# A hybrid decoder layer in fp32: the sum of two weight tiles of w_out, w_up and w_down formed in SBUF instead of DRAM

## The chip, the cores and the metric

The kernel runs on one core of a Trainium2 chip. The metric is the device time in microseconds (us) of one execution. Before the change the median of three runs is 1453.36 us (1452.56 to 1453.89).

## What is computed

One decoder layer (Hymba style) on 256 tokens with a model width of 2048, everything in float32:

```
u   = rmsnorm(h, norm_mix_pre)
P   = u @ w_in                       # 2048 x 12320: z | x,B,C | dt | q | k | v
y   = concat(SSD(z, xBC, dt), attention(q, k, v))       # 256 x 4096
h   = h + rmsnorm(y @ w_out, norm_mix_post)             # w_out 4096 x 2048
hdn = relu(rmsnorm(h, norm_mlp_pre) @ w_up) ** 2        # w_up 2048 x 8192
h   = h + rmsnorm(hdn @ w_down, norm_mlp_post)          # w_down 8192 x 2048
```

The SSD part is a chunked state space scan with a short causal convolution, the attention a mixture of three dilations. The four large products with w_in, w_out, w_up and w_down make up most of the work; all their weights are read from DRAM once.

## The kernel before, in words

**Products in two parts.** TensorE multiplies in a reduced fp32 format (F32R). To keep float32 accuracy each operand is split into a rounded part hi and a remainder lo, and three products stand for one: hi·hi, lo·hi and hi·lo. For the weights the split is made on the way: a *raw* tile of 2 x 128 rows by 512 columns (512 KB) is loaded by SP, ScalarE writes hi (L147), VectorE writes lo (L148), and TensorE uses both. There are five buffers each of hi and lo (BUFS).

**Plain steps and sevens.** The kernel works on two blocks of 512 columns at a time (a *unit*), over steps k of 256 rows. A plain step (row_tiles, row_tile, L331 to L333) loads one raw tile for each column block and makes 12 products of 128 x 128 x 512 from each: 24 for the two. A *seven* (seven(), L386 to L420) does the same step by a scheme of Strassen and Winograd with seven block products instead of eight: 21 products. It needs sums of blocks of weights. With raw_a the tile of the first column block and raw_b that of the second (each of rows [:, 0] and [:, 1]), raw_b's first half must hold the sum of its two row blocks, and VectorE then forms

```
e[:, 1] = raw_a[:, 0] + raw_b[:, 0]
e[:, 0] = e[:, 1] - raw_b[:, 1]
t4      = e[:, 1] + raw_a[:, 1]
```

through add_in_line, whose instructions are recorded at L252. The first of them is called e1 in what follows. The helpers split_in_line and add_in_line chain the instructions: on VectorE and ScalarE each stands behind the one before it, in the order e1, e[:, 0], split of raw_a, t4, split of e, split of raw_b, split of t4.

**Where the sum of raw_b's rows comes from.** plan() (L265) writes the order of the steps of each unit, and enters every seven in the list pairs. next_pair() (L270) takes the next entry and has GpSimd (POOL) make the sum in DRAM: a copy of the first 128 x 512 block to one of five places in DRAM (L279), then a transfer of the second block that adds onto it (L280, accum_op). Each of these is 256 KB, and POOL waits for the first to land before it issues the second. This runs four pairs ahead (PAIRS_AHEAD). fetch() (L152) then loads the finished sum into raw_b's first half (L156) and the second row block, unchanged, into its second half (L157); any other raw tile is one transfer (L161). There are 87 sevens: 21 in the products with w_in (z, q and k, v), 12 in w_out, 28 in w_up and 26 in w_down.

**The ring of raw tiles.** fetch_next() (L212) gives out the raw tiles in turn: the four of the pool wp (RAWS) and those that a stage adds in room["raw"], which are tiles that are free there: two more in w_out (part of uc), four more in the first half of w_up (the mw tiles, from the ninth raw tile on, since the turn starts at -2 * RAWS), one more in the first half of w_down (mw2), three more in the second half of w_up (ha), five more in the second half of w_down (uc and ha). A raw tile is loaded again when its last reader (hi, lo or one of the sums) has ended; SP issues the loads in order and waits at each for its slot.

**The orders.** In w_up each unit has sevens at k = 1, 3, 4 and 6. In the first half of w_down the two units are (4, 6, 9, 10, 11 and 13 are sevens in the first, 4, 6, 9, 11, 13, 10 and 8 in the second):

```
plan(("down", 0), w_down, 0, (0,1,2,4,3,6,5,9,7,10,8,11,12,13), (4,6,9,10,11,13))
plan(("down", 0), w_down, 2, (0, 4, 1, 6, 2, 9, 11, 3, 13, 5, 10, 7, 8), (4, 6, 9, 11, 13, 10, 8))
```

so that most sevens have one plain step between them. The remaining steps of a unit (14 and 15, for instance) follow as plain steps. At the end of w_out and the start of w_up an order written out by hand (mix_to_up, L1115) holds all engines; there POOL makes four small powers (L1084).

Of the kernel before, what the change touches and what calls it, by code (L numbers as in the profile page):

```python
# [14 lines left out]
ALU = mybir.AluOpType  # L15

P = 128
# [21 lines left out]
NB = 512  # L39
KB = 2  # L40
# [37 lines left out]
def hymba_layer(ctx: ExitStack, tc: tile.TileContext, x, norm_mix_pre, w_in, conv_w, conv_b, dt_bias, a_log,  # L78
                d_skip, ssm_norm_w, w_out, norm_mix_post, norm_mlp_pre, w_up, w_down, norm_mlp_post,
                consts, out):  # L80
    nc = tc.nc
    w_in, w_out, w_up, w_down = w_in[0], w_out[0], w_up[0], w_down[0]
# [69 lines left out]
    def fetch(src, k0, c0, step=KB, into=None, pair=None):  # L152

        raw = wp.tile([P, KB, NB], F32, name="raw", bufs=RAWS) if into is None else into
        if pair is not None:
            nc.sync.dma_start(raw[:, 0], pair)  # L156
            loaded[:] = [nc.sync.dma_start(raw[:, 1], src[(k0 + 1) * P:(k0 + 2) * P, c0:c0 + NB])]  # L157
            return raw
        for j in range(0, KB, step):
            rs = slice((k0 + j) * P, (k0 + j + step) * P)  # L160
            loaded[:] = [nc.sync.dma_start(raw[:, j:j + step], src[rs, c0:c0 + NB].rearrange("(k p) n -> p k n", p=P))]  # L161
        return raw

    loaded = []
# [47 lines left out]
    def fetch_next(src, k0, c0, pair=None):  # L212

        turn = room["turn"]
        room["turn"] += 1
        n = turn % (RAWS + len(room["raw"])) - RAWS
        into = None if turn < 0 or n < 0 else room["raw"][n]
        with ExitStack() as order:
            for last in loaded if room.get("chain") else ():
                order.enter_context(tc.issue_after(last.ins))  # L220
            return fetch(src, k0, c0, into=into, pair=pair)
# [32 lines left out]
    pairs = []  # L254

    w_z, w_v, w_ups, w_downs = w_in[:, COL_Z:], w_in[:, COL_V:], [w_up[:, hf * 4096:] for hf in range(2)], [w_down, w_down[4096:]]
    orders = {}

    def order_of(ks, by_seven):
        return [(k, k in by_seven) for k in ks]  # L260

    def blocks_of(n):
        return n if isinstance(n, tuple) else (n * NB, (n + 1) * NB)

    def plan(name, src, n, order, by_seven):  # L265

        orders[name, n] = order_of(order, by_seven)
        pairs.extend((src, blocks_of(n), k) for k in order if k in by_seven)

    def next_pair():  # L270

        if not pairs:
            return
        src, (ca, c), k = pairs.pop(0)
        cb = slice(c, c + NB)
        d = places[len(paired) % len(places)]
        if len(paired) < len(places):
            nc.gpsimd.dma_start(d[:, 0:1], room["pairs"])
        nc.gpsimd.dma_start(d, src[k * KB * P:(k * KB + 1) * P, cb])  # L279
        nc.gpsimd.dma_start(d, src[(k * KB + 1) * P:(k * KB + 2) * P, cb], accum_op=ALU.add)  # L280
        paired.append((src, ca, k, d))
# [3 lines left out]

    def pair_of(src, ca, k):

        next_pair()
        s_, c_, k_, d = paired[turn_of["pair"]]
        assert (s_ is src) and (c_, k_) == (ca, k), (c_, k_, ca, k)  # L290
        turn_of["pair"] += 1
        return d
# [3 lines left out]
    def weights(src, k0, c0, fetch=fetch):  # L296

        with tc.high_priority(offset=AHEAD):
            raw = fetch(src, k0, c0)
            hi, lo = parts()  # L300
            if fetch is fetch_next:
                split_in_line(hi, lo, raw)
                return hi, lo
            line.clear()
            with ExitStack() as order:
                while behind:
                    order.enter_context(tc.issue_after(behind.pop().ins))
                split(hi, lo, raw)
        return hi, lo
# [76 lines left out]
    def seven(src, ca, cb, k, acc, more, first, last):  # L386
# [4 lines left out]
        with tc.high_priority(offset=AHEAD):  # L391
            raw_a = fetch_next(src, k * KB, ca)
            raw_b = fetch_next(src, k * KB, cb, pair_of(src, ca, k))
            e, t4 = sum_tile(), tmp()
            add_in_line(e[:, 1], raw_a[:, 0], raw_b[:, 0])
            add_in_line(e[:, 0], e[:, 1], raw_b[:, 1], ALU.subtract)
            hl_a = parts()
            split_in_line(*hl_a, raw_a)
            add_in_line(t4, e[:, 1], raw_a[:, 1])
            hl_e = parts()  # L400
            split_in_line(*hl_e, e)
            hl_b = parts()
            split_in_line(*hl_b, raw_b)
            hl_t = parts()
            split_in_line(*(v[:, 0] for v in hl_t), t4)
# [16 lines left out]
    def combine_new(dst, more):  # L422

        with tc.high_priority(offset=AHEAD):
# [6 lines left out]
            nc.vector.tensor_tensor(b[1], more[3], b[0], op=ALU.add)  # L431

    plan("z", w_z, 0, (0, 2, 4, 6, 1, 3, 5), (1, 3))
    plan("z", w_z, 2, (0, 2, 1, 4, 3, 6, 5), (1, 3, 5))
    qk_blocks = [(COL_Q + hb * NB, COL_K + hb * NB) for hb in range(3)]
    plan("qk", w_in, qk_blocks[1], (0, 2, 1, 4, 3, 5, 6), QK_SEVENS)
    plan("v", w_v, 0, range(7), V_SEVENS)
    plan("qk", w_in, qk_blocks[2], (0, 2, 1, 3, 4, 5, 6), QK_SEVENS)
# [513 lines left out]
    def keys_too(hb, pumps=(1,)):  # L952
        return queries(COL_Q + hb * NB, rbq, pumps), queries(COL_K + hb * NB, rbc, pumps)
# [76 lines left out]
    qk = [keys_too(0, (2, 1))]  # L1030
# [526 lines left out]
```

## Time and profile before

| | before |
|---|---|
| median of 3 runs | 1453.36 us |
| the profiled execution: span | 1451.4 us |
| TensorE (PE) busy | 1442.4 us, 99% |
| VectorE (DVE) busy | 1300.4 us, 90% |
| ScalarE (ACT) busy | 947.1 us, 65% |
| GpSimd (POOL) busy | 162.3 us, 11% |
| SP's transfers (q1) | 272.37 MB, 58.1% of 16 transfer engines' span |
| POOL's transfers (q0) | 45.63 MB, 15.7% |
| granted TensorE clock, mean | 0.999 |

The profile is of one execution, whose span of 1451.4 us is 2.0 us below the median of the runs. The stages overlap at their borders; by the issues of SP's transfers they run roughly so: w_in to 566 us, w_out from 568 to 745, the first half of w_up from 746, the first half of w_down from 918, the second half of w_up up to 1254, and the second half of w_down to 1422, with the output after it.

In the views, a line names the engine and the source line, then what it writes <- what it reads. Rows of a timeline begin with the start and the duration in us; "SPq" is SP's queue issuing a transfer, so its duration is that of the issue and not of the transfer. The time "to landing" is counted from the issue to the semaphore that tells of the data's arrival. Lists of waits give the total, the number and the longest. A wait in brackets at the end of a row is idle time of that engine just before it and what ended it.

### The profile page before, as it was taken

What the parts mean: (1) busy time and instruction counts of PE and PEld (TensorE: products, weight loads), DVE (VectorE), ACT (ScalarE), POOL (GpSimd) and SP (SyncE); (2) the same over time, 40 slices, a digit from 0 to 9 for tenths busy, and PEclk for the clock granted to TensorE, in tenths of its full rate; (3) what the DMA queues carried; (4) which work ended last, traced back from release to release, by engine and by line L of the source; (5) the groups of instructions that cost most, each with busy time, mean ns of one, the idle gap of its engine ahead of it and who ended that gap; (6) DMA issues with size and microseconds to landing.
All of it is one profiled execution on the core that took longest, in us unless ns stands there. A gap on an engine that the chain in (4) does not pass through costs nothing.

```text
span 1451.4 us, 20394 instructions
## 1 busy us (share of the span) xinstructions
PE 1442.4 (99%) x7042; PEld 1214.7 (84%) x7042; DVE 1300.4 (90%) x1881; ACT 947.1 (65%) x1351; POOL 162.3 (11%) x244
## 2 busy tenths in 40 slices
PE   9999999999999999999999999999999999999998
PEld 8888888888888888888888888888888888888886
DVE  7788888988999788689988999999889999999998
ACT  7577669665666666556657677656465776766664
POOL 0201110131111000010100011010111110101000
PEclk9999999999999999999999999999999999999999
DMA  8977656756898658588976798688888888788854
GB/s 267 272 219 222 189 175 187 239 170 195 231 253 248 196 127 244 173 270 257 280 225 217 210 311 240 203 221 251 249 255 279 255 245 247 210 293 265 248 179 160
DMA packets 172359, 332.97 MB, mean 229 GB/s; under 512 B 16048, under 2 KB 18976, under 8 KB 172256
## 3 DMA queue, kind: packets, MB, share of 16 engines
q1 hardware_dynamic: 144736, 272.37, 58.1%
q0 software_dynamic: 19648, 45.63, 15.7%
q10 hardware_dynamic: 7872, 13.68, 2.8%
q8 instruction: 55, 0.90, 0.3%
q14 instruction: 48, 0.39, 0.1%
HBM read 327.39 MB, written 49.84 MB: 260 GB/s over the span
## 4 chain that ended last, share of the span: by engine, by line
PE 76%; ACT 1%; DVE 1%; DMA 0%; issue 0%; ACTq 0%
PE acc L331 10%; PE acc L333 10%; PE acc L332 10%; PE acc L418 7%; PE acc L419 7%; PE acc L420 7%; PE acc L485 4%; PE ps L331 3%; PE ps L332 3%; PE ps L333 3%; PE ps L418 2%; PE ps L419 2%; PE ps L420 2%; PE acc L488 2%; PE acc L1463 1%; PE ps L938 0%
## 5 line engine op out<-in xcount | busy, mean ns | idle before, releaser
L148 DVE TENSOR_TENSOR lo<-raw,hi 128x1024 fp32r<-128x1024 f32 (+1 forms) x387 | 470.1, 1220 | 79.1 <-ACT hi L147 76.3
L147 ACT ACTIVATE hi<-raw 128x1024 fp32r<-128x1024 f32 (+1 forms) x387 | 404.2, 1050 | 204.2 <-PE acc L333 71.4
L485 PE MATMUL acc<-ua,hi 128*128 128x512 f32 x520 | 141.2, 401 | 0.1
L147 ACT ACTIVATE hi<-e 128x1024 fp32r<-128x1024 f32 x66 | 70.2, 1063 | 68.5 <-DVE e L252 62.7
L485 PEld LDWEIGHTS acc<-ua,hi 128*128 128x128 f32 x520 | 91.3, 189 | 14.2 <-ACT hi L147 0.2
L331 PE MATMUL acc<-hi,ua 128*128 128x512 f32 x228 | 90.6, 397 | 0.0
L332 PE MATMUL acc<-lo,ua 128*128 128x512 f32 x228 | 89.3, 392 | 0.0
L333 PE MATMUL acc<-hi,ua 128*128 128x512 f32 x228 | 89.2, 391 | 0.0
L331 PE MATMUL acc<-hi,sh 128*128 128x512 f32 x220 | 86.9, 395 | 0.0
L333 PE MATMUL acc<-hi,sl 128*128 128x512 f32 x220 | 85.8, 390 | 0.0
L332 PE MATMUL acc<-lo,sh 128*128 128x512 f32 x220 | 85.7, 390 | 0.0
L488 PEld LDWEIGHTS acc<-ua,lo 128*128 128x128 f32 x520 | 76.5, 190 | 8.9
L148 DVE TENSOR_TENSOR lo<-e,hi 128x1024 fp32r<-128x1024 f32 x66 | 80.5, 1220 | 0.0
L488 PE MATMUL acc<-ua,lo 128*128 128x256 f32 x520 | 78.8, 282 | 0.0
L419 PE MATMUL acc<-lo,ah 128*128 128x512 f32 x180 | 70.1, 390 | 0.0
L420 PE MATMUL acc<-hi,al 128*128 128x512 f32 x180 | 70.1, 390 | 0.0
L418 PE MATMUL acc<-hi,ah 128*128 128x512 f32 x180 | 70.1, 390 | 0.0
L485 PE MATMUL acc<-uc,hi 128*128 128x512 f32 x208 | 61.4, 405 | 0.0
L148 DVE TENSOR_TENSOR lo<-ha,hi 128x1024 fp32r<-128x1024 f32 x43 | 52.5, 1221 | 6.0 <-ACT hi L147 5.8
L147 ACT ACTIVATE hi<-ha 128x1024 fp32r<-128x1024 f32 x43 | 45.2, 1057 | 19.4 <-PE acc L333 12.4
L147 ACT ACTIVATE hi<-r 128x512 fp32r<-128x512 f32 x66 | 41.5, 629 | 20.8 <-PE acc L333 8.8
L418 PE MATMUL acc<-hi,ua 128*128 128x512 f32 x137 | 53.7, 392 | 0.0
(572 smaller groups left out, 3722.3 us busy)
## 6 DMA issues: line engine op xcount, KB each, us to landing
raw<-in_w_in_dram SPq DMA_DIRECT2D x154, 512.0 KB, 4.5
raw<-in_w_down_dram SPq DMA_DIRECT2D x69, 512.0 KB, 5.7
raw<-in_w_up_dram SPq DMA_DIRECT2D x65, 512.0 KB, 4.8
raw<-in_w_out_dram SPq DMA_DIRECT2D x38, 512.0 KB, 5.1
raw<-pair SPq DMA_DIRECT2D x57, 256.0 KB, 4.3
pair<-in_w_up_dram POOLq DMA_DIRECT2D x56, 256.0 KB, 5.4
pair<-in_w_down_dram POOLq DMA_DIRECT2D x52, 256.0 KB, 6.3
pair<-in_w_in_dram POOLq DMA_DIRECT2D x42, 256.0 KB, 5.5
```

The lines of the kernel that those rows point to most:

```text
L147: return (nc.scalar.activation(hi, src, AF.Copy), nc.vector.tensor_tensor(lo, src, hi.bitcast(F32), op=ALU.subtract))
L148: nc.vector.tensor_tensor(lo, src, hi.bitcast(F32), op=ALU.subtract))
L331: nc.tensor.matmul(dst[:, cs], a_h[:, r, ts], hi[:, j, cs], start=begin and j == 0, stop=False)
L332: nc.tensor.matmul(dst[:, cs], a_h[:, r, ts], lo[:, j, cs], start=False, stop=False)
L333: product[t] = nc.tensor.matmul(dst[:, cs], a_l[:, r, ts], hi[:, j, cs], start=False, stop=end and j == KB - 1)
L418: nc.tensor.matmul(dst, a_h, hi[:, j], start=own and first, stop=False)
L419: nc.tensor.matmul(dst, a_h, lo[:, j], start=False, stop=False)
L420: nc.tensor.matmul(dst, a_l, hi[:, j], start=False, stop=own and last)
L485: nc.tensor.matmul(acc[f], hi[:, j, f * P:(f + 1) * P], u(k0 + j), start=k0 + j == 0, stop=False, skip_group_check=True)
L488: nc.tensor.matmul(acc[f][:, 0], lo[:, j, f * P:(f + 1) * P], u(k0 + j)[:, 0], start=False, stop=k0 + j == NK - 1, skip_group_check=True)
L1463: nc.tensor.transpose(p[:, f * P:(f + 1) * P], r[:, f * P:(f + 1) * P], ident)
```

## The change

In the units of w_out, w_up and w_down the pairs are no longer entered in the list, and pair_of() returns the word "here" for them. fetch() then loads both row blocks of raw_b as they are, with two transfers of SP, and has POOL add the second row block, read once more from DRAM, onto raw_b's first half in SBUF. That adding transfer waits for the load that it adds to, and e1 and the other readers of raw_b's first half wait for it. The 21 sevens of w_in keep the sum in DRAM.

```diff
@@ def fetch
         raw = wp.tile([P, KB, NB], F32, name="raw", bufs=RAWS) if into is None else into
+        if pair == "here":
+            loaded[:] = [nc.sync.dma_start(raw[:, j], src[(k0 + j) * P:(k0 + j + 1) * P, c0:c0 + NB]) for j in range(KB)]
+            nc.gpsimd.dma_start(raw[:, 0], src[(k0 + 1) * P:(k0 + 2) * P, c0:c0 + NB], accum_op=ALU.add)
+            return raw
         if pair is not None:
@@ def plan
         orders[name, n] = order_of(order, by_seven)
-        pairs.extend((src, blocks_of(n), k) for k in order if k in by_seven)
+        if name in ("z", "qk", "v"):
+            pairs.extend((src, blocks_of(n), k) for k in order if k in by_seven)
@@ def pair_of
+        if src is not w_z and src is not w_v and src is not w_in:
+            return "here"
         next_pair()
```

## The prediction

> **What bounds the kernel now.** I read the page first, then the busy time by stage, then the lists of waits of POOL and SP, then the timelines of SP, VectorE and TensorE around single sevens. (A *seven* is one call of seven(), e1 its first VectorE instruction, L395's addition recorded at L252; B is the raw tile that holds the sum, its first half B0.)
>
> ```profile
> span 1451.4 us, 20394 instructions
> PE 1442.4 (99%) x7042; PEld 1214.7 (84%) x7042; DVE 1300.4 (90%) x1881; ACT 947.1 (65%) x1351; POOL 162.3 (11%) x244
> PE 76%; ACT 1%; DVE 1%; DMA 0%; issue 0%; ACTq 0%
> ```
>
> ```profile
> 600.00:1440.00 840.00, 839.74 (x3817) 696.57 (x3816) 781.47 (x1030) 536.40 (x674) 85.43 (x126) 1.00 0.80 241
> 935.00:1090.00 155.00, 155.00 (x693) 128.33 (x692) 142.79 (x180) 93.75 (x106) 17.64 (x26) 1.00 0.84 241
> ```
>
> The second fence has the window, its length, and the busy time of PE, PEld, DVE, ACT and POOL, the granted clock, the DMA share and GB/s. All 66 sevens that the change touches lie in 600 to 1440 us, and there TensorE is without work for 0.26 us, at full clock. So no transfer holds the kernel up in this stretch, and nothing that the change makes cheaper can give back more than that. What remains is whether it makes TensorE wait. VectorE is the engine just behind it: 142.79 of 155 us in the first half of w_down. What a late weight costs is set by how early VectorE is.
>
> ```profile
> POOL pair L280 <- DMA pair<-in_w_down_dram: 146.1, 26, 7.4
> SPq L156 <- DVE lo L148: 121.3, 59, 5.1
> ```
>
> POOL's wait between its copy and its adding transfer, 5.6 us each time (146.1/26), is waited out four pairs ahead of use and costs nobody. SP's load of the finished sum (L156) waits for VectorE to free the slot, not for the sum.
>
> **What the change removes.** For each of the 66 sevens, the copy to DRAM (L279) and the reading back (L156). That lightens the transfer engines, by less than the 0.80 share in the row above, and the time saved is bounded by the 0.26 us. The number of SP issues stays two per B. POOL loses one issue a seven; it has no other work beside these sevens but the four small powers of L1084 between w_out and w_up, so nothing is queued there that suffers. I cost all this at nothing.
>
> **What it adds.** Today the sum is ready long before, and e1 can start when one plain load of B0 has landed. Afterwards there is a chain: SP loads B0, POOL waits for its landing, issues the adding transfer, and only when that has landed may e1 start. Behind e1, in an order that the kernel fixes, stand on VectorE every lo of this seven, and ScalarE's split of B; behind those, TensorE and the slots that SP refills. So I need the length X of the adding transfer, the lead of VectorE over TensorE, and the time from B0's issue to e1.
>
> The trace has no adding transfer into SBUF. Its neighbours, asked by source line (L156 and L280) in 935 to 1090 us, as least, median and greatest time from issue to landing:
>
> ```profile
> L156 SPq DMA_DIRECT2D raw<-pair x12: 327/338/339, 940.5 to 1072.4; - x12
> DMA to landing us min/median/max: 2.7/3.9/5.6
> ...
> L280 POOL DMA_DIRECT2D pair<-in_w_down_dram x8: 802/810/817, 950.9 to 1034.5; - x8
> DMA to landing us min/median/max: 4.5/6.4/8.3
> ```
>
> The plain load of the same 256 KB into SBUF (3.9) is the lower end, the addition in DRAM (6.4) the upper. The first lacks the addition and POOL's 0.8 us of issue; the second writes DRAM and shares the engines with the copies that go away. Being no nearer to one, I take the middle, X = 5.15.
>
> Here the Trainium skill would differ: its page "DMA: Bandwidth & Descriptors", section "Anatomy of one DMA — SWDGE (gpsimd) path", fits a GpSimd transfer by about 2.0 us and its bytes over 436 GB/s, 2.6 us for 256 KB, and says that receipts from HBM are the slow ones. By it the round worked out below would be 9.4 us, under TensorE's 10.2, and the time that of the first rival. The trace's quickest L280 took 4.5, so it doesn't agree for additions in DRAM; none into SBUF is shown.
>
> **The loop in the first half of w_down.** The ring there has five slots, a seven takes two and the plain step between two sevens takes two: B0 of a seven goes into the slot of the raw_a before it, freed when VectorE's lo of raw_a ends.
>
> ```profile
> 972.35 0.69 DVE L252 TENSOR_TENSOR e<-mw,raw 128x512 f32<-128x512 f32 x1
> 973.68 1.22 DVE L148 TENSOR_TENSOR lo<-mw,hi 128x1024 fp32r<-128x1024 f32 x1
> 982.88 0.68 DVE L252 TENSOR_TENSOR e<-raw,mw 128x512 f32<-128x512 f32 x1
> ...
> 974.93 0.34 SPq L156 DMA_DIRECT2D mw<-pair  x1
> ...
> 968.13 0.39 PE L418 MATMUL acc<-hi,sh 128*128 128x512 f32 x1
> 978.33 0.39 PE L418 MATMUL acc<-hi,ah 128*128 128x512 f32 x1
> ```
>
> That lo ends at 973.68 + 1.22 = 974.90, and B0 is issued at 974.93. Now B0 has until 982.88, 7.95 us, and needs 3.9. Afterwards the round is: e1 to the end of lo 2.55, SP's reaction 0.03, load 3.9, two handovers (to POOL, to VectorE) 0.35 (an estimate, ten times SP's 0.03), X 5.15: 11.98 us from e1 to e1. TensorE's round, seven to seven, is 978.33 - 968.13 = 10.20. So each such round loses 1.8 us. By the orders of plan(), five in ("down", 0), 0 have one plain step between two sevens, and five in ("down", 0), 2: 10 x 1.8 = 18. VectorE's lead, from the end of lo (974.90) to TensorE's use (978.33), is 3.4 us and hides so much once. At the change of the two units:
>
> ```profile
> 1017.02 0.34 SPq L156 DMA_DIRECT2D raw<-pair  x1
> 1019.85 0.69 DVE L252 TENSOR_TENSOR e<-raw 128x512 f32<-128x512 f32 x1
> 1030.01 0.39 PE L418 MATMUL ps<-hi,sh 128*128 128x512 f32 x1
> ```
>
> e1 comes 2.8 us after B0's issue and would need 3.9 + 0.35 + 5.15 = 9.4, 6.6 late; but TensorE uses this seven 10.2 us after e1 instead of 6.0 (978.33 - 972.35), which hides 4.2: 2.4. This stage: 18 - 3.4 + 2.4 = 17.
>
> **The other stages**, by the same 9.4 us from B0's issue to e1. The first unit of w_up runs on the four slots of the pool until the wider ring begins:
>
> ```profile
> 801.30 0.34 SPq L156 DMA_DIRECT2D raw<-pair  x1
> 816.72 0.34 SPq L156 DMA_DIRECT2D raw<-pair  x1
> 822.89 0.33 SPq L156 DMA_DIRECT2D raw<-pair  x1
> 829.65 0.46 SPq L156 DMA_DIRECT2D mw<-pair  x1
> ...
> 807.54 0.69 DVE L252 TENSOR_TENSOR e<-raw 128x512 f32<-128x512 f32 x1
> 822.78 0.68 DVE L252 TENSOR_TENSOR e<-raw 128x512 f32<-128x512 f32 x1
> 829.20 0.69 DVE L252 TENSOR_TENSOR e<-raw 128x512 f32<-128x512 f32 x1
> 837.88 0.69 DVE L252 TENSOR_TENSOR e<-mw 128x512 f32<-128x512 f32 x1
> ```
>
> They have 6.2, 6.1, 6.3 and 8.2 us, and miss 3.2, 3.3, 3.1 and 1.2: 10.8, less the lead of 3.4, 7.
>
> ```profile
> 865.92 0.34 SPq L156 DMA_DIRECT2D mw<-pair  x1
> 880.39 0.69 DVE L252 TENSOR_TENSOR e<-mw 128x512 f32<-128x512 f32 x1
> ...
> 670.33 0.34 SPq L156 DMA_DIRECT2D raw<-pair  x1
> 678.94 0.70 DVE L252 TENSOR_TENSOR e<-raw 128x512 f32<-128x512 f32 x1
> ...
> 1097.97 0.34 SPq L156 DMA_DIRECT2D raw<-pair  x1
> 1102.66 0.69 DVE L252 TENSOR_TENSOR e<-raw 128x512 f32<-128x512 f32 x1
> ...
> 1278.24 0.34 SPq L156 DMA_DIRECT2D raw<-pair  x1
> 1283.87 0.69 DVE L252 TENSOR_TENSOR e<-raw 128x512 f32<-128x512 f32 x1 [0.46 <-DMA raw<-pair]
> ```
>
> On the wider rings B0 has 14.5 us (first pair of rows): nothing. The tightest of w_out has 8.6 (second): 0.8 late, inside the lead. The first seven of w_up's second half has 4.7 (third) and misses 4.7; VectorE comes from w_down with its lead used up, so I count 4. The first of w_down's second half has 5.6 (last) and misses 3.8, partly hidden: 2.
>
> Sum: 17 + 7 + 4 + 2 = 30 us on the profile's span, 1451.4 + 30 = 1481.4. The median of the runs shown, 1453.36, is 2.0 above that span: **1483.4 us**.
>
> With X = 3.9 the round is 10.7 and the same terms give 3 + 2 + 3 + 1 = 9, so 1462. With X = 6.4 it is 13.2, and they give 31 + 12 + 5 + 3, and 1 for w_out, 52, so 1505.
>
> **The rivals.** *Not slower: the addition is hidden.* The round of w_down costs nothing while it is at most 10.2 us, that is with X up to 3.4. Then only the unit beginnings lose a little, 0 to 3 us: 1453 to 1456. For it: nothing in the trace adds into SBUF, and the copies beside it go. Against: the trace's quickest addition took 4.5, and even plain loads take 3.9 at the median. (The Trainium skill's 2.6 us, above, would bring this about.) A chance of 0.10.
>
> *Every unit pays.* If the addition into SBUF is as long as the longest in DRAM, X = 8.3, the round is 15.1: 10 x 4.9 + 3 = 52 in w_down, about 20 in the first unit of w_up, 7 and 6 at the two beginnings, and w_out's units of six slots go over too, some 12: 97, 1550 us. Against it: 8.3 is an extreme beside copies. 0.06.
>
> *Faster.* Fewer bytes could only shorten waits before 600 us, where all but a few of TensorE's 9 us of idle time lie (1451.4 - 1442.4), as some of w_out's sums are made there now. A gain over 0.2% (2.9 us, about what a measurement can tell from no change) would need a third of it. 0.02.
>
> *The sums stay in DRAM after all*: no; plan() no longer enters these pairs, and pair_of returns before it asks for one.
>
> **How the numbers follow.** The forecast's case, X between 3.9 and 6.4, has 0.82: 1483, from 1462 to 1505. Either end of X can be passed somewhat, and my hiding of the lead is rough by a few us: 1460 to 1510. Outside lie the hidden case and the long one. Faster 0.02, same 0.10, slower 0.88.
>
> **What would show it.** Right: gaps of VectorE ahead of L252, ended by the adding transfer, above all in 935 to 1130 us and around 805 to 850; TensorE idle by as much less its lead; POOL's adding transfers of about 5 us; rounds of 12 us in the first half of w_down and unchanged 10.2 us rounds in the second; SP later by VectorE's delay. Wrong: an X under 3.4; waits in the wide rings of w_up; or an engine order other than today's, which I take as kept apart from the edit.

## The result

The changed kernel takes 1515.11 us (median of 4 runs, 1512.82 to 1517.41), against 1452.96 us for the kernel before in the same session (4 runs, 1452.37 to 1453.89). The ratio is 1.0427, with a 95% interval of 1.0414 to 1.0440: slower by 62 us, where 30 were forecast. The direction and the places were foreseen; the size was not, and the time lies above the range given.

The page of the changed kernel has these lines, in answer to those of before. The q0 line is POOL's queue, the HBM line the traffic of the device memory, the last line the chain of work that ended last:

```profile
span 1515.6 us, 20386 instructions
PE 1464.8 (97%) x7042; PEld 1219.1 (80%) x7042; DVE 1299.0 (86%) x1881; ACT 939.3 (62%) x1351; POOL 128.9 (9%) x178
...
q0 software_dynamic: 14368, 28.32, 10.7%
HBM read 310.09 MB, written 15.24 MB: 215 GB/s over the span
...
PE 19%; DMA 3%; DVE 2%; ACT 0%; issue 0%; SPq 0%; ACTq 0%; DVEq 0%
```

VectorE and ScalarE have as much work as before, in a longer span. POOL's queue moves 28.32 MB instead of 45.63, and the writes are down to 15.24 MB. All of this is cheaper, and none of it was what the end waited for. What changed is the last line. The chain that ended last was 76% TensorE; now the profile follows it back only to 1127 us, where it arrives at an adding transfer, and of the quarter of the span from there on, 3% are transfers and 2% VectorE. Its pieces at the end of the first half of w_down and at the start of w_up's second half (start, duration, what):

```profile
1127.04 4.81 DMA raw<-in_w_down_dram
1131.87 0.70 DVE e L256
...
1150.48 10.25 DMA raw<-in_w_up_dram x2
1160.75 0.70 DVE e L256
```

add_in_line's instructions are now recorded at L256, SP's two loads of raw_b at L156, POOL's adding transfer at L157, the splits as before at L147 and L148. Both times a transfer ends, and e1 (L256) starts 0.02 us later.

The busy time by stage (columns as in the prediction: window, length, PE, PEld, DVE, ACT, POOL, clock, DMA share, GB/s):

```profile
600.00:1504.00 904.00, 861.81 (x3814) 700.61 (x3813) 779.75 (x1025) 528.28 (x674) 58.62 (x70) 0.98 0.71 208
957.00:1140.00 183.00, 163.33 (x677) 128.20 (x676) 137.05 (x172) 86.45 (x102) 11.00 (x13) 0.95 0.61 179
1240.00:1340.00 100.00, 100.00 (x460) 82.78 (x458) 94.72 (x116) 73.05 (x90) 5.91 (x7) 1.00 0.73 206
```

In the first half of w_down (second row) TensorE is without work for 19.7 of 183 us, with transfer engines less busy than before (0.61 against 0.84) and VectorE idle for 46 us. In the second half of w_up, on its wider ring (third row), TensorE is never idle, though every seven there uses the adding transfer too.

Idle time isn't the whole loss. TensorE executes the same 7042 products as before and is busy 22.4 us longer for them (1464.8 against 1442.4). So its idle time grew by only about 42 of the span's 64 us. The trace's clock records hold six stretches between 600 and 1500 us, of 3.4 or 6.8 us each and 27.3 us in all, in which the granted clock was 0.50; between the same times the kernel before has none. One of them and the stretch behind it, in the columns above:

```profile
1123.80:1127.20 3.40, 3.40 (x9) 2.40 (x8) 3.33 (x6) 1.08 (x2) 0.16 (x1) 0.50 0.66 189
1127.20:1132.00 4.80, 4.80 (x22) 3.96 (x22) 3.39 (x6) 2.53 (x3) 0.68 (x1) 1.00 0.77 206
```

TensorE works on 9 products in 3.4 us of the first and on 22 in 4.8 us of the second.

The list of waits shows the same. VectorE's e1 waits for the landing (the profile names it in some rows and writes "issue" where it doesn't recognise it), and ScalarE, whose split of e stands behind e1, waits for VectorE 145.2 us instead of the 62.7 of before:

```profile
ACT hi L147 <- DVE e L256: 145.2, 45, 10.0
DVE e L256 <- issue: 30.1, 6, 7.1
DVE e L256 <- DMA raw<-in_w_down_dram: 26.5, 7, 7.5
```

**Where the 64 us of the span came from.** TensorE's instructions stand in the same order in both kernels, so the start of a seven's first product in one trace can be subtracted from that in the other. This *lateness* grows only at these places:

| place | lateness there, us | grown by | forecast |
|---|---|---|---|
| last seven of w_out | 736.7 -> 742.1: 5.4 | 5.4 | 0 |
| w_up, first unit, up to the second unit's first seven | 861.4 -> 878.6: 17.2 | 11.8 | 7 |
| first seven of w_down | 957.9 -> 975.2: 17.2 | 0 | 0 |
| w_down, first half, up to its last seven | 1085.8 -> 1134.3: 48.6 | 31.4 | 17 |
| w_up, second half, second seven | 1122.5 -> 1180.4: 57.9 | 9.3 | 4 |
| w_down, second half, first seven | 1294.0 -> 1352.0: 57.9 | 0 | 0 |
| w_down, second half, second seven | 1304.2 -> 1368.2: 64.0 | 6.1 | 2 |
| end | 64.3 | 0.3 | 0 |

The places are those of the prediction but for w_out; each of them cost 1.7 to 3 times what was forecast, and the two wide rings cost nothing, as forecast. By TensorE's gaps, the 31.4 us of w_down are 19.6 of additional idle time and 11.8 of slower products, and the 27.2 of the three beginnings (11.8, 9.3 and 6.1) are 18.6 and 8.7.

**One round of w_down.** From e1 to e1 in the second unit of the first half (timelines of VectorE, SP, POOL and TensorE):

```profile
1105.33 0.69 DVE L256 TENSOR_TENSOR e<-raw 128x512 f32<-128x512 f32 x1 [6.17 <-issue]
1107.80 0.68 DVE L256 TENSOR_TENSOR r<-e,raw 128x512 f32<-128x512 f32 x1
1108.54 0.82 SPq L156 DMA_DIRECT2D raw<-in_w_down_dram  x2
1112.39 0.85 POOL L157 DMA_DIRECT2D raw<-in_w_down_dram  x1 [13.72 <-ACT hi L147]
1119.87 0.69 DVE L256 TENSOR_TENSOR e<-raw 128x512 f32<-128x512 f32 x1 [6.25 <-issue]
...
1104.94 0.39 PE L425 MATMUL ps<-hi,ah 128*128 128x512 f32 x1
1118.46 0.39 PE L425 MATMUL ps<-hi,ah 128*128 128x512 f32 x1
```

TensorE's round is 1118.46 - 1104.94 = 13.52 us; it was 10.20. VectorE's is 14.54: 3.21 from e1 to SP's issue (which comes when the sum t4, r<-e,raw, has ended at 1108.48), 3.85 until POOL issues the adding transfer, and 7.48 until that has landed and e1 starts. During the last 6.25 us VectorE does nothing, because e1 stands at the head of its fixed order.

By source line, all the transfers of this stage (935 to 1140 us) from issue to landing, SP's loads first, then POOL's additions:

```profile
L156 SPq DMA_DIRECT2D raw<-in_w_down_dram x24: 328/383/436, 957.7 to 1123.5; - x24
DMA to landing us min/median/max: 3.1/3.4/7.9
```

```profile
L157 POOL DMA_DIRECT2D raw<-in_w_down_dram x12: 841/844/867, 962.0 to 1127.0; - x12
DMA to landing us min/median/max: 4.2/6.2/8.4
```

The quantity X of the prediction is 6.2 us at the median here, not 5.15: about what the same addition took in DRAM (6.4).

### The profile page after: what moved, and what is told of

Read it like the earlier page. It is cut to its first block, busy times and chain, and to the rows that moved or that the text cites. A ratio compares the mean times of both kernels' runs of the same rounds, so it can differ in the third digit from the quotient of the medians.

```text
span 1515.6 us, 20386 instructions
## 1 busy us (share of the span) xinstructions
PE 1464.8 (97%) x7042; PEld 1219.1 (80%) x7042; DVE 1299.0 (86%) x1881; ACT 939.3 (62%) x1351; POOL 128.9 (9%) x178
## 3 DMA queue, kind: packets, MB, share of 16 engines
q0 software_dynamic: 14368, 28.32, 10.7%
HBM read 310.09 MB, written 15.24 MB: 215 GB/s over the span
## 5 line engine op out<-in xcount | busy, mean ns | idle before, releaser
L148 DVE TENSOR_TENSOR lo<-raw,hi 128x1024 fp32r<-128x1024 f32 (+1 forms) x387 | 469.5, 1218 | 71.6 <-ACT hi L147 69.5
L147 ACT ACTIVATE hi<-raw 128x1024 fp32r<-128x1024 f32 (+1 forms) x387 | 402.5, 1048 | 173.7 <-PE acc L492 43.1
L147 ACT ACTIVATE hi<-e 128x1024 fp32r<-128x1024 f32 x66 | 70.1, 1061 | 154.9 <-DVE e L256 145.2
L339 PE MATMUL acc<-lo,ua 128*128 128x512 f32 x228 | 89.7, 393 | 0.0
L256 DVE TENSOR_TENSOR e<-raw 128x512 f32<-128x512 f32 x37 | 25.5, 688 | 71.5 <-issue 30.1
L148 DVE TENSOR_TENSOR lo<-e,hi 128x1024 fp32r<-128x1024 f32 x66 | 80.4, 1219 | 0.0
L426 PE MATMUL acc<-lo,ua 128*128 128x512 f32 x137 | 54.0, 394 | 3.8 <-DVE lo L148 3.6
L148 DVE TENSOR_TENSOR lo<-ha,hi 128x1024 fp32r<-128x1024 f32 x43 | 52.4, 1220 | 5.7 <-ACT hi L147 5.5
```

Source lines behind the costliest of these rows:

```text
L147: return (nc.scalar.activation(hi, src, AF.Copy), nc.vector.tensor_tensor(lo, src, hi.bitcast(F32), op=ALU.subtract))
L148: nc.vector.tensor_tensor(lo, src, hi.bitcast(F32), op=ALU.subtract))
L256: line["dve"] = nc.vector.tensor_tensor(dst, a, b, op=op)
L339: nc.tensor.matmul(dst[:, cs], a_h[:, r, ts], lo[:, j, cs], start=False, stop=False)
L426: nc.tensor.matmul(dst, a_h, lo[:, j], start=False, stop=False)
```

## The experiments

The theory, A: the cost is the added wait of e1 (X and its two handovers) wherever the ring and the order leave B0 too little time, and nothing elsewhere. The rivals: B, every seven pays about the same (62 us over 66 sevens, 0.94 each), for instance for the third transfer; C, that a second transfer follows the load at all, however quick it is. All ratios are to the kernel before, run beside it on the same chip; the edits are to the changed kernel.

**Only the first half of w_down.** The 53 other sevens go back to the sum in DRAM.

```diff
-        if name in ("z", "qk", "v"):
+        if name != ("down", 0):
@@ def pair_of
-        if src is not w_z and src is not w_v and src is not w_in:
+        if src is w_down:
```

> Only the 13 sevens of the first half of w_down add in SBUF, the other 53 as before in DRAM. Theory A (e1 waits for a chain of load, hand-over and adding transfer that is longer than what the ring of raw tiles leaves): in the profile of the change this stage alone brings 31 us (sevens late by 17.2 us at its start, 48.6 at its last seven), so about 1484 us, 1480 to 1487. Rival B (adding transfers into SBUF slow all other transfers, a cost for each seven, 62/66 = 0.94 us): 13 x 0.94 = 12, about 1465 us.

Measured: 1484.42 us (1483.97 to 1487.67), ratio 1.0222 (1.0206 to 1.0237). Three windows of its trace, before, in and after that stage:

```profile
600.00:900.00 300.00, 299.76 (x1391) 249.04 (x1390) 272.99 (x385) 193.84 (x271) 31.81 (x47) 1.00 0.82 248
935.00:1125.00 190.00, 170.51 (x711) 134.29 (x710) 145.24 (x183) 90.38 (x107) 11.23 (x13) 0.96 0.62 181
1140.00:1300.00 160.00, 159.40 (x726) 131.69 (x725) 152.92 (x190) 110.61 (x135) 21.16 (x31) 1.00 0.85 246
```

TensorE waits in this stage alone. 13 of 66 sevens cost 31.8 us, 2.4 each, half of the whole: B falls, and the stage's 31 us are its own, not the effect of what comes before it.

**The raw tiles of a seven in the other order.** raw_b is fetched before raw_a, so that B0 takes the slot that comes free earlier.

```diff
-            raw_a = fetch_next(src, k * KB, ca)
             raw_b = fetch_next(src, k * KB, cb, pair_of(src, ca, k))
+            raw_a = fetch_next(src, k * KB, ca)
```

> All 66 sevens add in SBUF as in the change, but raw_b is fetched before raw_a, so that B0 takes the slot that raw_a had and is issued 1.4 to 3.1 us sooner. Theory A: the round of the first half of w_down comes from about 13 us down to 10.2 to 10.7, the unit beginnings improve by 2 us each; 62 us shrink to 10 to 20: 1463 to 1473 us. Rival B (traffic): the transfers are the same ones, so 1510 to 1517 us.

Measured: 1474.61 us (1472.57 to 1475.28), ratio 1.0147 (1.0132 to 1.0162). The window over the first half of w_down:

```profile
935.00:1100.00 165.00, 162.68 (x717) 132.40 (x716) 144.74 (x183) 94.79 (x111) 10.99 (x13) 1.00 0.68 206
```

The adding transfers are as long as before (6.1 at the median here), as many, and as heavy; what the edit moves is their place in the queue, in all 87 sevens, and with it some other instructions of VectorE and ScalarE stand elsewhere. TensorE's order is unchanged. The stage's growth in lateness falls from 31.4 to 4.4 us (6.7 to 11.1), and the whole cost from 62 to 22. So it is the lead of B0's load that decides, as A says (in the tight rounds B0 is now issued 0.1 us after the e1 before it, or sooner, where it was 3.2), and the 40 us that come back weigh against B and C alike. It came out 1.6 us above what A gave.

**The transfer without the addition.** POOL's transfer only writes the second row block over the first: the sum is left out.

```diff
-            nc.gpsimd.dma_start(raw[:, 0], src[(k0 + 1) * P:(k0 + 2) * P, c0:c0 + NB], accum_op=ALU.add)
+            nc.gpsimd.dma_start(raw[:, 0], src[(k0 + 1) * P:(k0 + 2) * P, c0:c0 + NB])
```

> The second transfer of GpSimd into raw_b's first half is plain, without the addition: the sum is left out, the second row block overwrites the first. The chain of two transfers stays. Theory A with the addition as the long part: X falls from 6.2 us in the first half of w_down to about 4.4 (between SP's plain 3.4 and the adding one), and the cost from 62 to 20 to 30 us: 1475 to 1483 us. Rival C (X is set by GpSimd's queue and by sharing with the other loads, not by adding): X stays near 6, 1508 to 1517 us.

Measured: 1487.31 us (1486.20 to 1488.82), ratio 1.0237 (1.0222 to 1.0253), above A's 1475 to 1483 and far under C's. The same line and window as above, of this kernel:

```profile
DMA to landing us min/median/max: 3.0/4.0/6.3
```

2.2 us less in X (6.2 - 4.0) take 62.2 - 34.6 = 27.6 us off, 12.5 us for each microsecond: ten rounds of w_down and about three beginnings of stages, where X counts once each. That fits A's mechanism. But A's size was off: an X of 4.0 would cost about 10 us by the prediction's terms, and costs 35. Of these, 14 are in w_down (9.3 to 23.3), the other 21 at w_out's end and at the beginnings.

**Half of the addition.** Only columns 0 to 255 of the second row block are added; the other half of the sum is left out.

```diff
-            nc.gpsimd.dma_start(raw[:, 0], src[(k0 + 1) * P:(k0 + 2) * P, c0:c0 + NB], accum_op=ALU.add)
+            nc.gpsimd.dma_start(raw[:, 0, :NB // 2], src[(k0 + 1) * P:(k0 + 2) * P, c0:c0 + NB // 2], accum_op=ALU.add)
```

> The adding transfer adds only columns 0 to 255 of the second row block (half of the sum is left out); still 128 rows, half the bytes. Theory A with the adding of bytes as the part that makes X 6.2 where a plain transfer has 4.0: X about 5.1 in the first half of w_down, and the time half way between the plain one (1487) and the change (1515): 1498 to 1506 us. Rival (a cost by rows or descriptors, or by the second trip itself): X stays at 6, 1511 to 1517 us.

Measured: 1496.71 us (1489.11 to 1499.44), ratio 1.0294 (1.0266 to 1.0323), just under A's 1498. The profiled run is the quickest of the four, 1489.11.

```profile
DMA to landing us min/median/max: 3.0/4.2/7.4
```

128 KB added take 4.2 us and 256 KB take 6.2; 256 KB written plainly take 4.0. A's X of about 5.1 was too long. The 2.2 us aren't a fixed price of every adding transfer, since half of the bytes were added in about the time in which all were written plainly. That the additional time is proportional to the bytes isn't shown: no run writes 128 KB plainly.

**The addition from SBUF.** The second row block is not read a second time from DRAM; POOL's transfer adds raw_b's second half, already in SBUF, onto its first. (The "third reading" below is raw_b's third transfer from DRAM. The second row block of every seven is read twice in the kernel before too, once for the sum and once as it is, so not all weights are read only once.)

```diff
-            nc.gpsimd.dma_start(raw[:, 0], src[(k0 + 1) * P:(k0 + 2) * P, c0:c0 + NB], accum_op=ALU.add)
+            nc.gpsimd.dma_start(raw[:, 0], raw[:, 1], accum_op=ALU.add)
```

> As the change, but the adding transfer takes the second row block from raw_b's second half in SBUF instead of reading it from DRAM once more; it waits for both loads. Theory A with the adding itself as what makes X long (half the bytes added took 4.2 us, all of them 6.2): X stays at 5.8 to 6.4 us and the time at 1508 to 1519 us. Rival (the third reading of DRAM makes X long): X falls toward 5 or below, 1485 to 1502 us.

Measured: 1520.02 us (1518.57 to 1523.24), ratio 1.0466 (1.0448 to 1.0483). By the time the rival falls: without that reading the kernel is no quicker, and even 1 us above A's range. The lengths tell it less simply, and nearer to the rival. In 935 to 1140 us the additions took

```profile
DMA to landing us min/median/max: 3.2/5.1/7.0
```

about 1.1 us less than from DRAM, so the reading from DRAM is part of X. But POOL now waits for both loads and issues 1.26 us after B0's landing instead of 0.56 (medians over the 66), and in the second unit of w_down, where it counts most, four of the five rounds with one plain step between still had 6.3 to 7.1 us (6.4 to 8.4 in the changed kernel). The lateness grows there by 23.0 us (28.8 to 51.8), against 22.5. So a part of X is the reading from DRAM, and some of what it gives back goes into the later issue; why X stays long in the second unit is open.

**GpSimd adds instead of a transfer.** One GpSimd instruction on the two loaded halves.

```diff
-            nc.gpsimd.dma_start(raw[:, 0], src[(k0 + 1) * P:(k0 + 2) * P, c0:c0 + NB], accum_op=ALU.add)
+            nc.gpsimd.tensor_tensor(raw[:, 0], raw[:, 0], raw[:, 1], op=ALU.add)
```

> No third transfer: GpSimd itself adds raw_b's second row block onto the first in SBUF, one instruction of 128x512, about 2.0 us by the 984 ns of its 128x256 in L830; it waits for both loads (0.6 us more). Theory A: e1 waits for load + 0.6 + 0.3 + 2.0 instead of load + 0.6 + 6.2; the round of w_down's first half is about 9.4 us, below 10.2; only unit beginnings lose a little: 1453 to 1459 us. Rival D (any second step behind the load, however short, uses up VectorE's lead): over 1465 us.

Measured: 1495.44 us (1493.66 to 1498.11), ratio 1.0292 (1.0275 to 1.0309). A's number failed, for a reason that it didn't contain, and the time lies in D's range. The groups by source line, a window, and a timeline of GpSimd and VectorE:

```profile
L157 POOL TENSOR_TENSOR raw<-raw x42: 1282/1612/3794, 625.2 to 1423.9; 128x512 f32<-128x512 f32 x42
L157 POOL TENSOR_TENSOR uc<-uc x6: 1285/1622/6902, 614.7 to 1438.1; 128x512 f32<-128x512 f32 x6
```

```profile
600.00:1484.00 884.00, 858.13 (x3818) 694.74 (x3817) 829.41 (x1027) 524.61 (x674) 127.15 (x70) 1.00 0.61 193
```

```profile
1353.34 0.29 DVE L386 TENSOR_TENSOR r<-r 128x128 f32<-128x128 f32 x1
1353.65 1.29 POOL L157 TENSOR_TENSOR raw<-raw 128x512 f32<-128x512 f32 x1 [10.70 <-DVE r L386]
1353.67 1.42 DVE L387 TENSOR_TENSOR r<-r 128x128 f32<-128x128 f32 x1
```

The same small addition of VectorE takes 0.29 us alone and 1.42 beside GpSimd's, and GpSimd's takes 1.28 us alone and up to 6.9. VectorE is busy for 829.41 us over the stretch in which it had 781.47 before: 48 us more on the engine with the least slack after TensorE. The chain in w_down is cured (14.4 to 19.8: 5.4 us instead of 31), which D doesn't explain, and time is lost in the wide rings too, where the changed kernel loses none. e1 also waits for GpSimd's addition itself, 12 times and 21.3 us in all; how the loss divides between these waits and VectorE's longer work isn't settled. The Trainium skill says it on its page "SBUF — State Buffer", section "Who interferes with whom": a VectorE instruction with both inputs in SBUF contends with a GpSimd instruction that reads SBUF. This trace agrees.

**The two beginnings.** The first seven of w_up's second half and the first of w_down's second half keep the sum in DRAM, the others as changed.

```diff
+    def in_dram_first(src, ca, k):
+        return src is w_z or src is w_v or src is w_in or (src is w_ups[1] and (ca, k) == (0, 1)) or (src is w_downs[1] and (ca, k) == (0, 3))
...
+        pairs.extend((src, blocks_of(n), k) for k in order if k in by_seven and in_dram_first(src, blocks_of(n)[0], k))
...
+        if not in_dram_first(src, ca, k):
```

> As the change, but the first seven of w_up's second half and the first of w_down's second half take their sum from DRAM, two of 66. Theory A with a loss at the beginnings of stages: the steps of 9.3 and 6.1 us there in the profile of the change go: 1515 - 15 = 1500, 1498 to 1503 us. Rival B (a cost for each seven): 2 x 0.94 = 2 us less: 1513 us.

Measured: 1501.11 us (1499.12 to 1503.49), ratio 1.0334 (1.0318 to 1.0349). The steps there are gone: from 44.2 to 45.0 us of lateness at the first, from 46.0 to 46.0 at the second. Without these two sevens the kernel is 14 us quicker.

**Only sevens that have cover.** 27 sevens in SBUF: w_up's first half but for its first unit, its second half but for the first unit, and the second unit of w_down's second half.

```diff
+    def in_dram_first(src, ca, k):
+        return not ((src is w_ups[0] and ca >= 4 * NB) or (src is w_ups[1] and ca >= 2 * NB) or (src is w_downs[1] and ca == 2 * NB))
```

> Only the 27 sevens add in SBUF that stand on wide rings past the beginnings (second and third unit of w_up's first half, second to fourth unit of its second half, second unit of w_down's second half); the other 39 take their sum from DRAM. Theory A: e1 waits at none of these, no loss: 1452 to 1455 us. Rival B (0.94 us for each seven): 27 x 0.94 = 25: 1478 us. No gain either way, since TensorE has no idle time to give back there.

Measured: 1453.70 us (10 runs, 1452.65 to 1458.12), ratio 1.0011 (1.0001 to 1.0020).

```profile
600.00:1440.00 840.00, 839.33 (x3814) 695.91 (x3813) 781.32 (x1028) 536.11 (x674) 72.22 (x99) 1.00 0.78 233
```

27 additions into SBUF cost 1 us in all, where B would have 25. VectorE's order is that of the kernel before here, instruction by instruction. They don't gain anything either: TensorE was idle for 0.26 us in this window before, and is idle for 0.67 now.

**VectorE's work at the beginnings.** At the start of w_up's second half e1 waits, and behind it in VectorE's order stands work that the sevens before it need, such as the emptying of an accumulator (L1429), for which TensorE then waits (timelines of VectorE and TensorE in the changed kernel):

```profile
1160.75 0.69 DVE L256 TENSOR_TENSOR e<-raw 128x512 f32<-128x512 f32 x1 [7.36 <-DMA raw<-in_w_up_dram]
1165.56 0.69 DVE L1429 TENSOR_TENSOR mw<-acc,mw 128x512 f32<-128x512 f32 x1
...
1166.40 0.47 PE L425 MATMUL acc<-hi,ah 128*128 128x512 f32 x1 [1.60 <-DVE mw L1429]
1171.22 0.47 PE L425 MATMUL acc<-hi,ah 128*128 128x512 f32 x1 [3.20 <-DVE mw L1429]
```

So the emptying was given a higher priority, to stand earlier on VectorE:

```diff
-            nc.vector.tensor_tensor(m, acc, m, op=ALU.subtract if n % 2 else ALU.add)
+            with tc.high_priority(offset=2 * AHEAD): nc.vector.tensor_tensor(m, acc, m, op=ALU.subtract if n % 2 else ALU.add)
```

> As the change, but in w_down's first half the instructions that empty a unit's banks (L1429, onto) have a higher priority, so that some of them stand a few places earlier on VectorE; they still come behind e1. Theory A with work queued behind e1 as the cause of the large steps at the beginnings: w_up's second half begins with a step of 6 to 8 instead of 9.3 us; in all 2 to 5 us less than the change: 1510 to 1513 us. Rival (the lateness of the weights alone): 1515 us as before.

Measured: 1517.61 us (1515.62 to 1521.04), ratio 1.0455 (1.0437 to 1.0472). In the profiled run this step is 6.7 us (48.2 to 54.9) instead of 9.3, as A had it, but the median did not fall. The two emptyings still stand behind e1, 3.5 and 5.3 us after its start instead of 4.8 and 9.6. TensorE no longer waits for them at all (4.80 us in the rows above), but its waits for the splits of weights (lo, L148) grew there from 1.68 to 4.30 us. So the emptying holds TensorE up for part of this step, and more than half of what is taken off it comes back as a wait for the late weights. The profiled run is the quickest of the four, and what the others lost, no trace shows.

**Both remedies.** raw_b first, and the first unit of w_up and the two beginnings back in DRAM: 60 sevens in SBUF.

```diff
+    def in_dram_first(src, ca, k):
+        return src is w_z or src is w_v or src is w_in or (src is w_ups[0] and ca == 2 * NB) or (src is w_ups[1] and (ca, k) == (0, 1)) or (src is w_downs[1] and (ca, k) == (0, 3))
...
-            raw_a = fetch_next(src, k * KB, ca)
             raw_b = fetch_next(src, k * KB, cb, pair_of(src, ca, k))
+            raw_a = fetch_next(src, k * KB, ca)
```

> raw_b is fetched before raw_a, and six sevens take their sum from DRAM: the four of the first unit of w_up and the first of the second halves of w_up and w_down; the other 60 add in SBUF. Theory A, terms that add up by place: with raw_b first the sevens ended 21.6 us late, of which 3.4 + 2.8 came at the start of w_up, 5.7 and 3.3 at the two beginnings; 6.4 are left: 1459 us, 1457 to 1463. Rival (a loss taken away at a beginning comes back at the next seven on the same rings): 1465 to 1475 us.

Measured: 1461.03 us (1458.93 to 1463.68), ratio 1.0058 (1.0043 to 1.0073). 60 of 66 sevens use the adding transfer, and 8 of 62 us are left, all in the first half of w_down (lateness 0.1 to 8.8; with raw_b first alone the growth there was 4.4). The sum comes out within A's range, but the places are not quite independent: w_down costs 4.3 us more here, where nothing was lost before it. No version here beats the kernel before.

## Why the prediction was right in direction and wrong in size

**What bounds the kernel.** Right. The lightened traffic (34.6 MB less written, loads in w_down landing in 3.4 us instead of 3.9) gave nothing, and the only question was whether TensorE would be made to wait.

**The chain through e1.** Right in kind: the gaps stand on VectorE ahead of e1, in the stages named; those with wider rings lose nothing. The experiment with raw_b first shows it most directly, since it leaves number, size and length of the transfers as they were and returns 40 us. The prediction took the engines' orders for unchanged. TensorE's is, but on VectorE a few instructions stand elsewhere around the change of units and at the beginnings of the two second halves; what that weighs was not tested.

**The failed step: X.** "Being no nearer to one, I take the middle, X = 5.15." It was 6.2 at the median in the first half of w_down, by the row above, and there was a reason to be nearer to the upper row: that one adds 256 KB too, and the adding makes the transfer long (6.2 against 4.0). By the Trainium skill's fit ("DMA: Bandwidth & Descriptors", "Anatomy of one DMA — SWDGE (gpsimd) path") an estimate for these 256 KB is 2.6 us; it lies under the least of the plain transfer (3.0) as well as of the adding one (4.2), beside this kernel's other loads.

**The round.** Forecast 2.55 + 0.03 + 3.9 + 0.35 + 5.15 = 11.98; by the medians of the stage it is 3.2 (e1 to SP's issue) + 3.2 (B0's landing) + 0.6 (to POOL's issue) + 6.2 + 0.05 = 13.3. Besides X, the first term was mis-sized: the round that the prediction read had raw_a in an mw tile, whose first half came free when lo had ended; in rounds on the pool's tiles the slot comes free only when t4 has ended, 0.6 us later. The handover to POOL was 0.6, not a part of 0.35. The quicker load gave 0.7 back. In the first unit six e1 stand 12.7 us apart (968.64 to 1032.09, five rounds), in the second the five rounds with one plain step between have 13.6, 15.4, 14.5, 14.5 and 12.0, a mean of 14.0. Against TensorE's 10.2 that is 5 x 2.5 = 12.5 in the first and 5 x 3.8 = 19.0 in the second. The change of units adds 2.8 (23.9 between the two e1, against TensorE's 21.1 before; forecast 2.4), and the round without a plain step 1.2, which the prediction left out. Of these 35.4 the stage shows 31.4: 4.0 are hidden, about the forecast lead of 3.4. Why X is longer in the second unit (a median of 6.6 against 5.4) is open.

**The beginnings.** The second failed step: 13 us forecast (7 + 4 + 2), 27 measured (11.8 + 9.3 + 6.1). X is longer than assumed there as well (7.7 and 8.2 us at the two first sevens, beside loads that took up to 10 and 8). But the run without the addition still has 21 us of them and of w_out, so it isn't X alone: the prediction set the lateness of e1 against the lead of this seven, and behind e1 VectorE also holds work for products already under way, which has hardly any lead. At the first seven of w_up, VectorE waits 4.20 us ahead of e1, and rbc, a small copy that stands behind it, comes 3.69 us after e1 as it did before (3.68); TensorE waits for rbc:

```profile
818.42 0.69 DVE L256 TENSOR_TENSOR e<-raw 128x512 f32<-128x512 f32 x1 [4.20 <-DMA raw<-in_w_up_dram]
822.11 0.42 DVE L653 COPY rbc<-ps 128x256 f32<-128x256 f32 x1
...
822.67 0.63 PE L1361 MATMUL ps<-ident,r 128*128 128x128 f32 x4 [3.84 <-DVE rbc L653]
```

With the 1.60 and 3.20 us for the emptying above, 8.6 of the 27 us are waits of TensorE for such work. By the run with the emptying moved, not all of them would be saved without it.

**A term that is missing: slower products.** The prediction found TensorE at full clock and added up nothing but waits. TensorE's idle time is 42 of the 64 us; the other 22 are slower products. Of the half-clock stretches, those at 823.4 and 1171.6 begin right behind the waits of 3.84 and 3.20 us; the one at 1086.2 has no wait in the 16 us ahead of it, so what sets them off is open. One can argue that in a round that waits for e1 anyway slower products only fill part of the wait, and that behind the last wait of a beginning they come on top. How much they add in all isn't shown, since no run kept the clock up.

**w_out.** Forecast 0, measured 5.4: the "0.8 late, inside the lead" rested on X = 5.15. At 6.2 it would still be inside, but in w_out the additions took 4.1 to 10.2, and the loads ahead of them up to 7.0; the first seven of its second unit, with 9.3, brought 3.4 us.

**The rivals.** *Hidden*: with an X of 4.0, not far from its bound of 3.4, 35 us are still lost, 21 of them outside w_down, so the 0 to 3 us that it gave the beginnings were far too low; the bound came from w_down's round alone. *Every unit pays*: three of the 66 transfers had 8.3 us or more (8.4, 9.3 and 10.2), and the wide rings stayed covered, TensorE busy for 100.00 of 100 us at 1240. *Faster*: the bytes saved shortened no wait that counted.

**How much each failed step weighs.** The prediction's terms give 30 us at X = 5.15 and 52 at 6.4, so about 48 at 6.2. Of the 34 us by which the span was missed, X makes 18 by these terms, and the other terms 16, the beginnings and w_out above all. The upper end, 1510, came from X = 6.4 with those other terms kept and a few us for the hiding of the lead; they were taken from single rows, and the range held nothing more for them.

## What to carry to other kernels

Work taken out of a stage that runs far ahead and put into the path from a buffer's release to its first reader is paid once per round of the ring, and the price is the whole chain less what the ring leaves, not the work's cost. An instruction that waits on an engine with a fixed order delays all that stands behind it, and some of that has no lead, so a stage's beginning costs more than the lead of the waiting item suggests. A third of the loss here was not idle time of TensorE but slower products, so a sum of waits is too small. For an operation that the trace doesn't show, take the neighbour that does the same thing, and vary every term of the round for the range, not one.

## What the runs showed of the hardware

- A POOL transfer that adds 256 KB into SBUF took 6.2 us at the median in the first half of w_down, plainly writing them 4.0, adding 128 KB 4.2, adding 256 KB that lie in SBUF 5.1; adding them in DRAM had taken 6.4 in the kernel before (935 to 1090 us). POOL's issue took 0.84 us, and came 0.56 us after the landing that it waited for.
- VectorE and GpSimd instructions with two inputs in SBUF held each other up: VectorE's addition of 128x128 took 0.29 us alone and 1.42 beside GpSimd's, GpSimd's of 128x512 1.28 us alone and up to 6.9.
- Where TensorE waited in each round, its granted clock was lower: 0.95 in 957 to 1140 us, against 1.00 in 1240 to 1340, where it did not wait. It fell to 0.50 for 3.4 or 6.8 us at a time, and products of 128x512 took 0.63 us there instead of 0.39 (at 1172.34 and at 1176.09, for instance).
